# An average pool on one core: the first tile's load cut into eight transfers of 16 interleaved partitions

## The chip, the cores and the metric

The kernel runs on one core of one Trainium2 chip; its other cores are idle. The metric is the time of one execution on the device in microseconds (us), lower is better. Before the change three runs gave 334.86, 334.95 and 335.12 us, with a median of 334.95 us.

## The reference

The input x has 32 batches of 256 channels of 4096 float32 values (134.2 MB). Each row of 4096 is cut into 256 windows of 16, and each window is averaged, so the output has 32 x 256 x 256 float32 values (8.4 MB).

```python
result = np.zeros((batch, channels, output_size), dtype=np.float32)
for i in range(output_size):
    start = int(i * length / output_size)
    end = int((i + 1) * length / output_size)
    result[:, :, i] = np.mean(x[:, :, start:end], axis=-1)
```

## The kernel before, in words

Batches and channels are put together into 8192 rows of 16 KB. The kernel works through them in 16 tiles of 512 rows: 128 partitions with R = 4 rows each, so that a tile is 128 x 16384 float32 values, 8.39 MB, and each partition takes one unbroken run of 64 KB from memory. The first 15 tiles share a layout (`x_many`) in which partition p owns 60 successive rows of x and tile t takes the t-th four of them. The last tile has a layout of its own (`x_last`).

Per tile, in program order:

- SP, the engine that issues the transfers, issues the load of the tile `xin` (line 64) as one transfer over all 128 partitions. The pool `inpool` has two buffers, so tile t can't be loaded before tile t-2 has been worked off.
- POOL (line 67) adds the upper eight to the lower eight elements of each window, for the second half of the tile's windows (`m` to `cells`, 512 windows in each partition).
- DVE sums the first half's windows of 16 (line 72), and then the second half's windows of 8 that POOL has left (line 75). Both write into `res_many`, or for the last tile into `res_last`. Line 75 is the last reader of the tile, and with it the buffer comes free.
- ACT scales the tile's results by 1/16 in place (line 78).

The results of the first 15 tiles stay in `res_many` and are stored by one transfer (line 66) that SP issues behind the last load, once ACT has scaled tile 14. The last tile's results are stored at the end (line 83). All transfers, loads and stores, go through SP's one queue to the core's 16 DMA engines, in the order in which SP issues them. POOL and DVE wait for the whole tile, by the semaphores of its transfers. The framework gives each transfer one of eight semaphores in turn, and where a semaphore comes round again, it has SP wait until its last transfer has landed.

Of the kernel before, what the change touches and what calls it, by code (L numbers as in the profile page):

```python
# [1 line left out]

# [4 lines left out]


@with_exitstack
def kernel(  # L10
    ctx: ExitStack,
    tc: tile.TileContext,
    x: bass.AP,
    output_size: int,
    out: bass.AP,
):

    nc = tc.nc
    F32 = mybir.dt.float32
    X = mybir.AxisListType.X

    batch, channels, length = x.shape
    ob, oc, olen = out.shape
    assert ob == batch and oc == channels and olen == output_size
    assert length % output_size == 0
    window = length // output_size  # L30
    hw = window // 2
    inv_w = 1.0 / float(window)

    P = nc.NUM_PARTITIONS
    R = 4
    rows = batch * channels
    assert rows % (P * R) == 0
    ntiles = rows // (P * R)
    many = (ntiles - 1) * R
    cells = R * output_size  # L40
    m = cells // 2
    cols = R * length

    xr = x.rearrange("b c l -> (b c) l")
    orow = out.rearrange("b c o -> (b c) o")
    x_many = xr[0 : P * many, :].rearrange("(p r) l -> p (r l)", p=P, r=many)
    o_many = orow[0 : P * many, :].rearrange("(p r) o -> p (r o)", p=P, r=many)
    x_last = xr[P * many :, :].rearrange("(p r) l -> p (r l)", p=P, r=R)
    o_last = orow[P * many :, :].rearrange("(p r) o -> p (r o)", p=P, r=R)

    inpool = ctx.enter_context(tc.tile_pool(name="inpool", bufs=2))
    respool = ctx.enter_context(tc.tile_pool(name="respool", bufs=1))
    res_many = respool.tile([P, (ntiles - 1) * cells], F32, name="res_many")
    res_last = respool.tile([P, cells], F32, name="res_last")

    for t in range(ntiles):
        last = t == ntiles - 1
        xin = inpool.tile([P, cells, window], F32, name="xin")
        if last:
            res, base, src = res_last, 0, x_last  # L60
        else:
            res, base = res_many, t * cells
            src = x_many[:, t * cols : (t + 1) * cols]
        nc.sync.dma_start(out=xin.rearrange("p o w -> p (o w)"), in_=src)  # L64
        if last:
            nc.sync.dma_start(out=o_many, in_=res_many[:, :])
        nc.gpsimd.tensor_add(  # L67
            out=xin[:, m:cells, 0:hw],
            in0=xin[:, m:cells, 0:hw],
            in1=xin[:, m:cells, hw:window],  # L70
        )
        nc.vector.reduce_sum(  # L72
            out=res[:, base : base + m], in_=xin[:, 0:m, :], axis=X
        )
        nc.vector.reduce_sum(  # L75
            out=res[:, base + m : base + cells], in_=xin[:, m:cells, 0:hw], axis=X
        )
        nc.scalar.mul(  # L78
            out=res[:, base : base + cells],
            in_=res[:, base : base + cells],  # L80
            mul=inv_w,
        )
    nc.sync.dma_start(out=o_last, in_=res_last[:, :])


# [1 line left out]
_INS = ['x', 'output_size']  # L87
_OUTS = [((32, 256, 256), 'float32')]

_NUMBERS = {'output_size': 256}  # L90


# [26 lines left out]
```

## Time and profile before

| | |
|---|---|
| median of three runs | 334.95 us |
| the profiled execution: time | 334.98 us |
| the profiled execution: span from first to last instruction | 333.2 us |
| data moved | 134.22 MB read, 8.39 MB written |
| DMA engines busy, share of the span | 99.1% |
| DVE, POOL, ACT busy | 209.7, 139.7, 18.2 us |
| packets on the DMA queue | 2592, of them 288 under 512 B |

The span lacks 1.8 us of the execution's own time. A packet is what one DMA engine moves in one piece: each of the 16 loads and the two stores has 128 data packets, one for each partition, and one small packet on each of the 16 engines that counts up the semaphore, together 18 x (128 + 16) = 2592. "Landing" is the moment when the last of these has arrived. In the chain of waits, "DMA" is time in which the chain waits for a landing. "SPq" and "POOLq" are those engines' sequencers, and "issue" is time with no wait that the profile shows.

### The profile page before, as it was taken

Reading aid. Unit: us, or ns where it says so; the run is one execution under the profiler, and the core shown is the slowest. Engines: PE = TensorE matmul, PEld = TensorE weight load, DVE = VectorE, ACT = ScalarE, POOL = GpSimd, SP = SyncE. Lnnn points to the kernel's source line nnn. Section 1 sums busy time; section 2 is a strip of 40 time slices with the busy share of each in tenths; the row PEclk is TensorE's granted clock in tenths of the full one; section 3 lists DMA queues with packets and bytes.
Section 4 is the critical chain, followed back from the end, with each engine's and each line's share of the span. In section 5 each row is a group of like instructions: output and inputs, shape, how many; then the busy total and the mean of one; then the engine's idle time right before and its main releaser. Section 6 shows DMA issues by size and latency. Waiting matters only on the chain.

```text
span 333.2 us, 158 instructions
## 1 busy us (share of the span) xinstructions
DVE 209.7 (63%) x32; ACT 18.2 (5%) x17; POOL 139.7 (42%) x20
## 2 busy tenths in 40 slices
DVE  0029396693929569392956839295783929578491
ACT  1000101001010100001010000101010010101001
POOL 0027091642709064370906336090733609073460
DMA  9898989999898989999898989989898989989896
GB/s 378 378 504 378 496 386 456 425 417 464 378 504 378 496 386 472 409 425 456 378 504 378 504 378 456 425 378 504 378 504 378 504 378 456 425 386 496 384 450 299
DMA packets 2592, 142.61 MB, mean 428 GB/s; under 512 B 288, under 2 KB 288, under 8 KB 416
## 3 DMA queue, kind: packets, MB, share of 16 engines
q1 hardware_dynamic: 2592, 142.61, 99.1%
HBM read 134.22 MB, written 8.39 MB: 428 GB/s over the span
## 4 chain that ended last, share of the span: by engine, by line
DMA 66%; POOL 18%; DVE 11%; POOLq 3%; issue 0%; ACT 0%; SPq 0%
DMA xin<-in_x_dram 66%; POOL xin L67 18%; DVE res_many L75 9%; POOLq L114 3%; DVE res_last L75 1%; ACT res_last L78 0%; SPq L64 0%; POOLq L67 0%
## 5 line engine op out<-in xcount | busy, mean ns | idle before, releaser
L67 POOL TENSOR_TENSOR xin<-xin 128x4096 f32<-128x4096 f32 x16 | 139.5, 8717 | 181.9 <-DMA xin<-in_x_dram 181.9
L72 DVE TENSOR_REDUCE res_many<-xin 128x512 f32<-128x8192 f32 x15 | 130.3, 8686 | 107.9 <-DMA xin<-in_x_dram 107.9
L75 DVE TENSOR_REDUCE res_many<-xin 128x512 f32<-128x4096 f32 x15 | 66.3, 4420 | 2.5 <-POOL xin L67 2.3
L78 ACT ACTIVATE res_many<-res_many 128x1024 f32<-128x1024 f32 x15 | 15.8, 1056 | 290.2 <-DVE res_many L75 290.2
L72 DVE TENSOR_REDUCE res_last<-xin 128x512 f32<-128x8192 f32 x1 | 8.7, 8687 | 6.1 <-DMA xin<-in_x_dram 6.1
L75 DVE TENSOR_REDUCE res_last<-xin 128x512 f32<-128x4096 f32 x1 | 4.4, 4420 | 0.2 <-POOL xin L67 0.2
L78 ACT ACTIVATE res_last<-res_last 128x1024 f32<-128x1024 f32 x1 | 1.1, 1056 | 18.3 <-DVE res_last L75 18.3
L78 ACT ACT_TABLE_LOAD x1 | 1.3, 1283 | 0.7 <-PEq L100 0.7
L100 POOL MEMSET const-float32-0.0<- 128x1 f32 x1 | 0.1, 98 | 0.2 <-issue 0.2
L100 POOL MEMSET const-bfloat16-1.0<- 128x1 bf16 x1 | 0.1, 101 | 0.0
L100 POOL MEMSET const-uint8-127<- 128x1 uint8 x1 | 0.1, 101 | 0.0
L100 POOL MEMSET const-float32-1.0<- 128x1 f32 x1 | 0.1, 98 | 0.0
## 6 DMA issues: line engine op xcount, KB each, us to landing
out_dram<-res_many SPq DMA_DIRECT2D x1, 7680.0 KB, 23.0
out_dram<-res_last SPq DMA_DIRECT2D x1, 512.0 KB, 4.9
xin<-in_x_dram SPq DMA_DIRECT2D x16, 25.4
```

Of the source, the lines that this page charges most:

```text
L67: nc.gpsimd.tensor_add(out=xin[:, m:cells, 0:hw], in0=xin[:, m:cells, 0:hw], in1=xin[:, m:cells, hw:window],)
L72: nc.vector.reduce_sum(out=res[:, base : base + m], in_=xin[:, 0:m, :], axis=X)
L75: nc.vector.reduce_sum(out=res[:, base + m : base + cells], in_=xin[:, m:cells, 0:hw], axis=X)
L78: nc.scalar.mul(out=res[:, base : base + cells], in_=res[:, base : base + cells], mul=inv_w,)
L100: nc = _bacc.Bacc("TRN2", target_bir_lowering=False, num_devices=1)
L114: with _tile.TileContext(nc) as tc:
```

## The change

The load of tile 0 becomes eight transfers in place of one. Transfer j takes the partitions j, j+8, j+16 and so on up to j+120: 16 of the 128 partitions, one 64 KB run in each. All other loads stay as they are, and so do all instructions of POOL, DVE and ACT.

```diff
     R = 4
+    STEP = 8
...
-        nc.sync.dma_start(out=xin.rearrange("p o w -> p (o w)"), in_=src)
+        flat = xin.rearrange("p o w -> p (o w)")
+        if t == 0:
+            for j in range(STEP):
+                nc.sync.dma_start(out=flat[j:P:STEP, :], in_=src[j:P:STEP, :])
+        else:
+            nc.sync.dma_start(out=flat, in_=src)
         if last:
             nc.sync.dma_start(out=o_many, in_=res_many[:, :])
```

In the compiled program SP's list has eight copies of 16 x 16384 ahead of fifteen of 128 x 16384. The eight take all eight semaphores. So the load of tile 1, which had no wait, now waits for the first of the eight to land; the load of tile 2 waits for the other seven and, as before, for DVE; and the first instructions of POOL and of DVE wait for eight semaphores in place of one. Elsewhere the order of each engine's instructions is the same.

## Prediction

> **What bounds the kernel now.** I read the chain of waits by line first, then the two busy rows over the span, then stretches of time, and last the waits of SP and of the engines.
>
> ```profile
> DMA xin<-in_x_dram 66%; POOL xin L67 18%; DVE res_many L75 9%; POOLq L114 3%; DVE res_last L75 1%; ACT res_last L78 0%; SPq L64 0%; POOLq L67 0%
> DMA  9898989999898989999898989989898989989896
> DMA packets 2592, 142.61 MB, mean 428 GB/s; under 512 B 288, under 2 KB 288, under 8 KB 416
> q1 hardware_dynamic: 2592, 142.61, 99.1%
> ```
>
> The chain gives POOL 18% and DVE 9%, because it passes through the work that frees a buffer. The other rows say that the DMA engines are busy for 99.1% of the span, so they are the real bound. The stretches (columns: DVE, ACT, POOL busy; granted clock; DMA share; GB/s, where a packet counts at its start, so that short stretches can show a share over 1):
>
> ```profile
> 1.00:1.50 0.50, 0.00 (x0) 0.50 (x1) 0.00 (x0) 1.00 0.00 0
> 1.50:2.00 0.50, 0.00 (x0) 0.50 (x1) 0.00 (x0) 1.00 4.38 1442
> 2.00:2.25 0.25, 0.00 (x0) 0.01 (x1) 0.00 (x0) 1.00 2.28 786
> 2.25:2.50 0.25, 0.00 (x0) 0.00 (x0) 0.00 (x0) 1.00 0.70 262
> 2.50:2.75 0.25, 0.00 (x0) 0.00 (x0) 0.00 (x0) 1.00 0.74 262
> ...
> 42.09:61.44 19.35, 13.11 (x2) 1.06 (x1) 8.72 (x1) 1.00 1.00 434
> 61.44:293.67 232.23, 157.27 (x24) 12.67 (x12) 104.61 (x12) 1.00 1.00 433
> ```
>
> The queue starts between 1.5 and 2.75 us and then never rests. One load takes 19.35 us (DVE starts on tile 1 at 42.09 and on the last two tiles at 293.67 and 313.02 us). An engine moves 8 of the 128 runs in that time: 19.35 / 8 = 2.42 us for a run of 64 KB, 27.1 GB/s for each engine, 16 x 27.1 = 433 GB/s. So whatever makes one engine's line of runs longer or shorter, anywhere, moves the end by as much, unless it is less than the cover named below.
>
> **The change, part by part.**
>
> *Seven more issues on SP.* One issue of line 64 takes 328 ns as a median and 425 at most, by that line's own view; eight take 8 x 0.38 (the first one's row in the chain) = 3.0 us, against one 0.38 before. The run of transfer j is wanted by its engine only when j earlier runs are through, 2.42 us apart, and an issue takes 0.38. The queue therefore fills faster than it drains, and this costs 0. Without that cover it would be 7 x 0.38 = 2.7 us.
>
> *Semaphore packets.* 7 x 16 = 112 more, seven on each engine. The packet records of the trace, one level below the views, put each at 9 ns, and the next run starts 6 ns after it begins: 7 x 6 to 7 x 9 ns = 0.04 to 0.06 us. I take 0.05.
>
> *The start.* The stretches show 1442 GB/s x 0.5 us = 0.72 MB, or 11 runs, starting before 2.0 us, then 3, 1 and 1: 16 runs, the last 0.8 us behind the first (the records have them from 1.70 to 2.48). The last engine stays last to the end. If the descriptors of a transfer are made engine after engine, 16 runs of a small transfer are handed out sooner than 128. Bounds: a gain between 0 and 0.78 us. The trace has no transfer of this form; I take 0.15, because the early starters' first runs lasted longest (up to 3.5 us, the late ones 2.8 to 3.0), so that most of the head start was not kept.
>
> *New waits.* SP:
>
> ```profile
> SPq L64 <- DVE res_many L75: 185.8, 14, 13.3
> SPq L64 <- DMA xin<-in_x_dram: 95.3, 14, 21.2
> ```
>
> Load 1 was issued straight behind load 0; now it waits for the first of the eight, which lands about one run after the start, 1.7 + 3.1 = 5 to 7 us even if a run takes twice as long. Its own runs are wanted only when load 0 is through, at 21.7 us or later: 0, with 15 us of cover. Behind it on SP stands load 2, which waits for DVE anyway. POOL and DVE start tile 0 behind eight semaphores; a wait of this kind took 17 ns on SP and POOL's steps before its adds 0.02 and 0.09 us, so seven more are 0.1 to 0.8 us at the most, and those for early transfers pass while the last one is still under way. This delays the freeing of tile 0's buffer (35.97 us: line 75 starts at 31.55 and takes 4.42) and so the issue of load 2. But load 1 keeps the queue busy until 41 us or so (DVE starts on it at 42.09), a cover of 5 us: 0.
>
> *The run's own length.* This is the open price. Every transfer of the trace spans all 128 partitions; none shows 16 runs of which each lies eight partitions from the next. Lower bound: such a run takes 2.42 us as its nearest kin in size do, and the price is 0; nothing below, since no stretch of the trace exceeds 434 GB/s. Upper bound: the 27.1 GB/s is not the engine's pace but that of an entrance of the on-chip memory which several partitions share, and two runs of a small transfer meet in one entrance: 2 x 2.42 = 4.84 us, a load of 8 x 4.84 = 38.7 us, and a price of 19.35 us with no cover, as the DMA engines have no slack. In size the nearest row is the 2.42; in what differs, which partitions are written at once, there is no row. I take the upper end, and that is a choice. For it: the pace is the same to a per mille with every run of 230 us, which is how a fixed path looks and not a memory with traffic. For it, weakly: the only runs that set out nearly in step, the first ones, took up to 3.5 us, a few tenths of a run of which may be a start-up delay. Against it: all rows agree with an engine's own limit as well. The selection is regular, every eighth, and a regular selection meets a regular division of the memory either evenly or with whole groups left out; half of them is the least that can be left out by a step of eight over a division in powers of two.
>
> [...] The stretches show 434 GB/s with 128 partitions in one transfer. [...]
>
> **The sum.** The profiled execution's own time, 334.98 us (span 333.2 and 1.8 around it): 334.98 + 19.35 + 0.05 - 0.15 = 354.2 us. It lies 0.03 above the median of the runs, so **354.2** stands. Behind tile 0 nothing is new: load 2 is again issued some 5 us before it is wanted, all shifted by 19.35 us.
>
> **The rivals.**
>
> - *Forecast, runs doubled:* 354.2 us, 352.5 to 355.5. Chance 0.70.
> - *Fewer engines:* a small transfer is not one run per engine but sits on eight of the 16, always the same ones, two runs each at 2.42 us. The change then doesn't do what it says, and the load again takes 16 x 2.42 = 38.7 us: 354.2 as well, but with a DMA share near 0.5 in tile 0. Chance 0.03.
> - *Partly shared:* one of two engines gets ahead until they no longer meet, or they meet on half the runs: a price of about 9.7 us, 340 to 351. Chance 0.09.
> - *No sharing (the other side):* the mechanism is that a run goes at its engine's own pace wherever it lands. Place: the 8 runs of each engine in tile 0. Price 0: 334.98 + 0.05 - 0.15 = 334.9. It decides as soon as a run of a small transfer takes under 2.42 + 0.67 / 8 = 2.50 us. For it: every one of the 2304 long and short runs fits. Chance 0.14.
> - *No sharing, and a start in step:* the whole 0.78 us is won: 334.98 + 0.05 - 0.78 = 334.25, which is just over 0.2% faster. Chance 0.04.
>
> **How the numbers follow.** 0.2% is 0.67 us, about what a measurement of this kernel can tell from no change. Faster 0.04; within 0.2% 0.14; slower 0.70 + 0.03 + 0.09 = 0.82. The likeliest case's own range is 352.5 to 355.5. The range must take in both ends of the open price, so it runs from the no-sharing case, 334.4, to the doubled one, 355.5.
>
> **What would show it.** In the profile after: DVE's first start (22.76 us before) at about 42; the DMA share in the first 40 us still near 1 while GB/s there is near 217, which is sharing, or a share near 0.5, which is fewer engines; 19.35 us per tile from then on; SP's load of tile 1 issued by 7 us and the DMA share without a gap before tile 2. A first start of DVE near 22.5 would make the prediction wrong at the run's length; a gap after tile 0 would make it wrong at the waits. The packet count should be 2592 + 112 = 2704.

## The result, and the profile after

The changed kernel takes 356.19 us (median of five runs, 356.16 to 356.36) against 334.95 us for the kernel before, run beside it: a ratio of 1.0634 (95% interval 1.0618 to 1.0649). It is 21.2 us slower; the span of the profiled execution grew from 333.2 to 354.4 us. The forecast was 354.2 us, with a range that ended at 355.5.

The page of the changed kernel: the chain by line, the DMA share and the rate in 40 slices, the packets.

```profile
DMA xin<-in_x_dram 61%; POOL xin L74 20%; DVE res_many L82 9%; POOLq L121 2%; DVE res_last L82 1%; SPq L69 1%; ACT res_last L85 0%; POOLq L74 0%
DMA  9979998999999999999999999999999999999996
GB/s 237 207 148 237 237 451 377 473 436 392 473 436 392 473 436 392 473 414 414 473 407 422 473 407 422 473 399 429 473 392 436 473 392 436 473 392 436 459 444 281
DMA packets 2704, 142.61 MB, mean 402 GB/s; under 512 B 400, under 2 KB 400, under 8 KB 528
```

The share of busy time shows almost nothing: the engines are as busy as before (99.2% of the span, 99.1% before). The rate beside it shows all of it: in the first five slices (44 us) it is half, and then it is back. A run counts as busy time for as long as it takes, so runs that last twice as long leave the share at 1. The same by stretches (columns as in the prediction):

```profile
2.00:2.25 0.25, 0.00 (x0) 0.01 (x1) 0.00 (x0) 1.00 12.28 2621
2.25:2.50 0.25, 0.00 (x0) 0.00 (x0) 0.00 (x0) 1.00 7.60 1573
...
10.00:20.00 10.00, 0.00 (x0) 0.00 (x0) 0.00 (x0) 1.00 1.02 210
20.00:30.00 10.00, 0.00 (x0) 0.00 (x0) 0.00 (x0) 1.00 1.01 210
30.00:40.00 10.00, 0.00 (x0) 0.00 (x0) 0.00 (x0) 1.00 1.02 210
...
64.00:314.00 250.00, 169.79 (x26) 13.73 (x13) 112.80 (x13) 1.00 1.00 433
```

The kernel before, from 10 to 40 us:

```profile
10.00:40.00 30.00, 13.11 (x2) 1.06 (x1) 8.72 (x1) 1.00 0.99 428
```

Between 2.00 and 2.50 us 2621 x 0.25 + 1573 x 0.25 = 1049 KB start, which is 16 runs of 65.5 KB: all 16 engines have one at once. From 10 to 40 us the share is 1 and the rate 210 GB/s. The packet records, one level below the views, show the runs of load 0 at 5.10 us (2.42 before), except the fifth on each engine at 4.91 us and the first, which took 4.39 to 5.35 us. The timeline, with start, duration, engine and line:

```profile
0.73 4.98 SPq L69 DMA_DIRECT2D xin<-in_x_dram  x8
8.59 49.39 SPq L71 DMA_DIRECT2D xin<-in_x_dram  x2
44.41 8.69 DVE L79 TENSOR_REDUCE res_many<-xin 128x512 f32<-128x8192 f32 x1 [44.41 <-DMA xin<-in_x_dram]
63.42 8.69 DVE L79 TENSOR_REDUCE res_many<-xin 128x512 f32<-128x8192 f32 x1 [5.80 <-DMA xin<-in_x_dram]
```

The same two starts of DVE in the kernel before:

```profile
22.76 8.69 DVE L72 TENSOR_REDUCE res_many<-xin 128x512 f32<-128x8192 f32 x1 [22.76 <-DMA xin<-in_x_dram]
42.09 8.69 DVE L72 TENSOR_REDUCE res_many<-xin 128x512 f32<-128x8192 f32 x1 [6.12 <-DMA xin<-in_x_dram]
```

DVE starts on tile 0 at 44.41 us in place of 22.76. On tile 1 it starts at 63.42 in place of 42.09, later by 21.3 us, and that is the delay of the end. Behind tile 1 everything is as it was, with 433 GB/s and 19.35 us to a tile.

### The profile page after: what moved, and what is told of

The parts are those of the page before. It is cut to its first block, busy times and chain, and to the rows that moved or that the text cites. A ratio compares the mean times of both kernels' runs of the same rounds, so it can differ in the third digit from the quotient of the medians.

```text
span 354.4 us, 176 instructions
## 1 busy us (share of the span) xinstructions
DVE 209.7 (59%) x32; ACT 18.2 (5%) x17; POOL 139.7 (39%) x20
## 3 DMA queue, kind: packets, MB, share of 16 engines
q1 hardware_dynamic: 2704, 142.61, 99.2%
## 4 chain that ended last, share of the span: by engine, by line
DMA 61%; POOL 20%; DVE 10%; another core or an unknown queue 3%; POOLq 3%; SPq 1%; issue 0%; ACT 0%
DMA xin<-in_x_dram 61%; POOL xin L74 20%; DVE res_many L82 9%; POOLq L121 2%; DVE res_last L82 1%; SPq L69 1%; ACT res_last L85 0%; POOLq L74 0%
```

## The experiments

Three theories stood against each other. **Shared entrances** (the forecast's): several partitions share one way into the on-chip memory, and two engines whose runs meet there halve each other. No trace shows such an entrance, so the theory is judged by the rates and run lengths that it foresees. **Transfer count**: eight transfers with their semaphores cost a stall each. **Source rows**: the distance in memory between the 16 runs of a transfer (7.9 MB) slows the reading. Each experiment changes only the loop that loads tile 0.

### Sixteen neighbours to a transfer

```diff
-    nc.sync.dma_start(out=flat[j:P:STEP, :], in_=src[j:P:STEP, :])
+    nc.sync.dma_start(out=flat[16 * j : 16 * j + 16, :], in_=src[16 * j : 16 * j + 16, :])
```

> Tile 0 in eight transfers of 16 neighbouring partitions, from 16j to 16j + 15, in place of every eighth one. Three theories. Shared entrances: the runs of one transfer queue at the few entrances that its partitions share; with four runs to an entrance a run takes 4 x 2.42 = 9.7 us, or 4 x 2.55 = 10.2 us at the pace that the changed kernel's runs show (5.10 us for two), so tile 0 takes 77 to 82 us and the kernel 393 to 397 us. [...] Transfer count: each of the eight transfers costs its engines a stall, wherever its partitions lie: 356 us, as the changed kernel. Source rows: the 7.9 MB between a transfer's runs in memory is what slows it; here they are 0.98 MB apart as in the kernel before: 335 us.

Measured: 388.98 us, ratio 1.1612 (1.1591 to 1.1633). DVE's first start and the stretch before it:

```profile
77.29 8.69 DVE L81 TENSOR_REDUCE res_many<-xin 128x512 f32<-128x8192 f32 x1 [77.29 <-DMA xin<-in_x_dram]
10.00:66.00 56.00, 0.00 (x0) 0.00 (x0) 0.00 (x0) 1.00 1.03 116
```

The 116 GB/s at a full share (1.03) are about a quarter of 433. Eight transfers again, but 54 us slower instead of 21: the count is not the price. The source rows, at 0.98 MB as before, are not either. From the second on a run took 9.28 us, below the 9.67 that four runs to an entrance should give, so the size was missed. The four itself was the author's estimate; what the run shows is the quarter of the rate. The two experiments on the order, below, show where the difference lies: behind certain other sets a run is shorter, 4.91 us in place of 5.10 and 9.24 in place of 9.64. Such a run is called a passage here, because by the author's reading it goes to other entrances than the run before it; the records show its length alone.

### Two halves

```diff
-            for j in range(STEP):
-                nc.sync.dma_start(out=flat[j:P:STEP, :], in_=src[j:P:STEP, :])
+            for j in range(2):
+                nc.sync.dma_start(out=flat[64 * j : 64 * j + 64, :], in_=src[64 * j : 64 * j + 64, :])
```

> Tile 0 in two transfers, partitions 0 to 63 and 64 to 127. Shared entrances: each half reaches half of the entrances, so every run takes about 5 us, the load 8 x 4.84 to 8 x 5.10 = 39 to 41 us, the kernel 354 to 356 us. [...] Transfer count: one boundary in place of seven, 21.2 / 7 = 3.0 us: 338 us. Source rows: 0.98 MB apart as before: 335 us.

Measured: 356.31 us, ratio 1.0636 (1.0617 to 1.0656). DVE's first start:

```profile
44.29 8.69 DVE L81 TENSOR_REDUCE res_many<-xin 128x512 f32<-128x8192 f32 x1 [44.29 <-DMA xin<-in_x_dram]
```

Two transfers cost what eight cost, and the rate from 10 to 40 us was 210 GB/s again. That each half reaches half of the entrances was the author's estimate; the run shows half the rate. The runs took 5.12 us, the fifth, where the second half begins, 4.92 us.

### Eight transfers over all partitions

```diff
-    nc.sync.dma_start(out=flat[j:P:STEP, :], in_=src[j:P:STEP, :])
+    nc.sync.dma_start(out=flat[:, j * c : j * c + c], in_=src[:, j * c : j * c + c])
```

Here `c` is an eighth of the 16384 columns.

> Tile 0 in eight transfers again, but each over all 128 partitions and an eighth of the columns (2048 of 16384, runs of 8 KB). The number of transfers, their semaphores and all waits are those of the changed kernel; only the set of partitions is the whole one. Shared entrances: 334.9 to 335.5 us, the price of the seven further transfers alone (some 0.05 us for their semaphore packets, and what the longer runs list adds at the start). Transfer count: 356 us. Source rows: 335 us.

Measured: 335.21 us, ratio 1.0007 (0.9998 to 1.0016), no difference that can be told. The profile of this kernel:

```profile
13.25 8.69 DVE L82 TENSOR_REDUCE res_many<-xin 128x512 f32<-128x8192 f32 x1 [13.25 <-DMA xin<-in_x_dram]
10.00:40.00 30.00, 13.11 (x2) 1.06 (x1) 8.72 (x1) 1.00 1.06 451
```

The seven further transfers, their semaphores and the waits cost nothing visible. The cut by columns even lets DVE begin at 13.25 us, because its half of the tile is complete after four transfers, and that is worth nothing either: the DMA queue sets the end.

### The same partitions from one stretch of memory

```diff
-    nc.sync.dma_start(out=flat[j:P:STEP, :], in_=src[j:P:STEP, :])
+    nc.sync.dma_start(out=flat[j:P:STEP, :],
+                      in_=xr[64 * j : 64 * j + 64, :].rearrange("(p r) l -> p (r l)", p=16, r=R))
```

> Every eighth partition as in the changed kernel, but transfer j takes its 16 runs from one unbroken megabyte of x (rows 64j to 64j + 63) in place of runs 7.9 MB apart. Tile 0 then holds other rows of x than the reference puts there. Shared entrances and transfer count: 356 us, with runs of 5.1 us. Source rows: 335 us, with runs of 2.42 us; between the two if both matter.

Measured: 356.15 us, ratio 1.0632 (1.0612 to 1.0651).

```profile
44.51 8.69 DVE L82 TENSOR_REDUCE res_many<-xin 128x512 f32<-128x8192 f32 x1 [44.51 <-DMA xin<-in_x_dram]
```

The source of the runs doesn't matter; runs took 5.09 us. (Tile 0 holds other rows of x here, so the output is not the reference's; the amounts moved are the same.) Of the three theories only the one on the set of partitions that is written at once is left.

### Another order of the eight

```diff
-            for j in range(STEP):
+            for j in (0, 4, 1, 5, 2, 6, 3, 7):
```

> The eight transfers of the changed kernel in the order 0, 4, 1, 5, 2, 6, 3, 7 in place of 0 to 7. In the changed kernel all runs take 5.10 us but the fifth, which takes 4.91 us; it is the one at which j passes from 3 to 4. [...] In this order every run from the second on is such a passage: seven runs at 4.91 in place of one, so the load is 6 x 0.19 = 1.1 us shorter and the kernel takes 355.0 us. If the short fifth run has another cause, which goes by its place in the list, it stays the only one: 356.2 us.

Measured: 355.27 us, ratio 1.0608 (1.059 to 1.0625), so 0.9 us less than the changed kernel; the forecast of this experiment was 355.0.

```profile
43.33 8.69 DVE L79 TENSOR_REDUCE res_many<-xin 128x512 f32<-128x8192 f32 x1 [43.33 <-DMA xin<-in_x_dram]
```

DVE starts 1.1 us sooner than in the changed kernel (44.41). The records have nearly every run from the second on at 4.91 to 4.93 us (the longest 4.96). The short fifth run goes with the change from j below 4 to j from 4 on, not with its place. The author reads it as a change of entrances; the run shows the lengths.

### Every fourth and every second partition over the whole tile

```diff
-            for j in range(STEP):
-                nc.sync.dma_start(out=flat[j:P:STEP, :], in_=src[j:P:STEP, :])
+            for j in range(4):
+                nc.sync.dma_start(out=flat[j:P:4, :], in_=src[j:P:4, :])
```

> Tile 0 in four transfers of every fourth partition, 32 partitions each. [...] Shared entrances with engine e taking two successive partitions of the set (8e + j, 8e + 4 + j): at any time the 16 engines still write only half of the entrances, and change over at every run: runs of 4.91 us, 355 us. Shared entrances with each engine keeping to an entrance of its own: 2.42 us, 335 us. Cost by transfer or by the step in the partitions alone: between the two kernels, 335 + 3/7 x 21.2 = 344 us.

Measured: 335.34 us, ratio 1.0014 (1.0003 to 1.0024).

```profile
23.08 8.69 DVE L79 TENSOR_REDUCE res_many<-xin 128x512 f32<-128x8192 f32 x1 [23.08 <-DMA xin<-in_x_dram]
10.00:40.00 30.00, 13.11 (x2) 1.06 (x1) 8.72 (x1) 1.00 1.04 452
```

```diff
-            for j in range(STEP):
-                nc.sync.dma_start(out=flat[j:P:STEP, :], in_=src[j:P:STEP, :])
+            for j in range(2):
+                nc.sync.dma_start(out=flat[j:P:2, :], in_=src[j:P:2, :])
```

> Tile 0 in two transfers of every second partition, 64 partitions each. [...] Shared entrances with engine e taking four successive partitions of the set: two runs on one half of the entrances, two on the other; three passages at 4.91 us, the others at 5.10 us: 355.8 us. With each engine keeping to an entrance of its own: 335 us. A cost by transfer: 338 us.

Measured: 335.28 us, ratio 1.0012 (1.0002 to 1.0022).

```profile
22.96 8.69 DVE L79 TENSOR_REDUCE res_many<-xin 128x512 f32<-128x8192 f32 x1 [22.96 <-DMA xin<-in_x_dram]
```

Both run at the full rate (452 and 450 GB/s from 10 to 40 us), with runs of 2.42 us. So neither a step in the partitions nor part of the partitions is the trouble. If the entrances are shared, a set that reaches all of them must be dealt out so that engines don't meet; successive partitions of the set to one engine, the first reading of each expectation, is out. The two kernels take 0.4 to 0.5 us more than the kernel before. Part of it stands in the traces from the start: DVE begins tile 1 at 42.29 and 42.22 us in place of 42.09. The first run begins at 2.06 us in place of 1.73, and SP's first issue took 0.54 and 0.55 us in place of 0.38.

### Every fourth partition of one half

```diff
-            for j in range(STEP):
-                nc.sync.dma_start(out=flat[j:P:STEP, :], in_=src[j:P:STEP, :])
+            for h in (0, 64):
+                for j in range(4):
+                    nc.sync.dma_start(out=flat[h + j : h + 64 : 4, :], in_=src[h + j : h + 64 : 4, :])
```

> Tile 0 in eight transfers of 16 partitions, every fourth one of the lower 64 and then of the upper 64. [...] If a step of eight is what hurts: 335 us. [...]

Measured: 356.1 us, ratio 1.0634 (1.0613 to 1.0655).

```profile
43.94 8.69 DVE L82 TENSOR_REDUCE res_many<-xin 128x512 f32<-128x8192 f32 x1 [43.94 <-DMA xin<-in_x_dram]
10.00:40.00 30.00, 0.00 (x0) 0.00 (x0) 0.00 (x0) 1.00 1.02 210
```

With 16 partitions of 64, a step of four costs what a step of eight does over 128; with 32 partitions over all 128 it cost next to nothing. Nor does the number of partitions in a transfer decide: 64 neighbours took 356.31 us, 64 with a step of two 335.28. What counts is which partitions the set holds; that it counts by the entrances that the set reaches is the author's reading. A division into groups of eight neighbours that share an entrance is out: the changed kernel's transfers write one partition of each group, and their runs took 5.10 us all the same. The fifth run, with which the upper half begins, took 4.89 us on all 16 engines.

### Sixteen neighbours to a transfer, in another order

Against the kernel with 16 neighbours to a transfer (388.98 us, runs of 9.28 us from the second on):

```diff
-            for j in range(STEP):
+            for j in (0, 2, 1, 3, 4, 6, 5, 7):
```

> The eight blocks of 16 neighbouring partitions again, in the order 0, 2, 1, 3, 4, 6, 5, 7 in place of 0 to 7. [...] If four sharers cost nothing, 9.67 us: 390.5 us. If an entrance is faster than one engine, 9.28 us throughout: 389.0 us.

Measured: 390.9 us, ratio 1.1672 (1.1638 to 1.1706).

```profile
78.97 8.69 DVE L81 TENSOR_REDUCE res_many<-xin 128x512 f32<-128x8192 f32 x1 [78.97 <-DMA xin<-in_x_dram]
```

The second, fourth, sixth and eighth run took 9.64 us as a median, the third, fifth and seventh 9.24 to 9.25. The reading that came to 390.5 us holds: at a quarter of the rate a run takes four times 2.41 us, without a loss. The 390.5 counts four runs at 9.67 us in place of 9.28; that there are four was the author's estimate, and the records have four, at 9.64. The short runs stand where a block follows its neighbour (2 to 1, 3 to 4, 6 to 5); in the first order every block from the second on does, so its 9.28 us are read as passages.

### Shorter runs

```diff
+            h = cols // 2
             for j in range(STEP):
-                nc.sync.dma_start(out=flat[j:P:STEP, :], in_=src[j:P:STEP, :])
+                for c in (0, h):
+                    nc.sync.dma_start(out=flat[j:P:STEP, c : c + h], in_=src[j:P:STEP, c : c + h])
```

> The changed kernel's eight sets of every eighth partition, each in two transfers of half the columns: 16 transfers with runs of 32 KB in place of 64. It asks what the 0.26 us is by which a run of 5.10 us exceeds twice 2.42. If the entrance loses a share of its pace when two engines write to it, a run takes 2.55 us, the load is as long as before, 356.2 us. If each run pays it once, whatever its length, a run takes 2.42 + 0.26 = 2.68 us, and the kernel 356.2 + 8 x 0.26 = 358.3 us.

Measured: 356.15 us, ratio 1.0634 (1.0603 to 1.0665).

```profile
44.29 8.69 DVE L83 TENSOR_REDUCE res_many<-xin 128x512 f32<-128x8192 f32 x1 [44.29 <-DMA xin<-in_x_dram]
```

From the second on, runs of 32 KB took 2.55 to 2.57 us, except the passage (the ninth) at 2.38. The loss beyond twice 2.42 us is a share of the pace (5%), not a price for each run. Sixteen transfers cost what eight and two cost.

## Why the prediction was wrong, and where it was right

**The step that failed** is the upper bound of "the run's own length": "two runs of a small transfer meet in one entrance: 2 x 2.42 = 4.84 us". It took sharing to be free of loss, so what was called a bound was none. Measured: seven runs of 5.10 and one of 4.91 us, 40.6 us in place of 38.7. This alone is 1.9 us and puts the time past the range's end of 355.5. The half of the rate that the mechanism foresaw was there: 210 GB/s at a share of 1.01 to 1.02. But no run shows an entrance, nor that two runs meet in one; what the runs showed in place of the 4.84 us are these lengths.

The sum, against the records of the engine that ended load 0 last:

| term | predicted, us | measured, us |
|---|---|---|
| runs of load 0: 7 x 5.10 + 4.91 - 8 x 2.42 | +19.35 | +21.25 |
| start-up in the first run (2.96 - 2.42 before, 5.35 - 5.10 after) | not in the sum | -0.29 |
| this engine's start (2.51 before, 2.30 after) | -0.15 | -0.21 |
| seven more semaphore packets, by the gaps between the runs | +0.05 | +0.04 |
| first run of load 1 (2.42 before, 2.78 after) | not in the sum | +0.36 |
| sum | +19.25 | +21.15 |

The start of load 2's first run on this engine is later by 21.15 us, as the sum has it, and the end of the kernel by 21.2. All terms but the first differ from the prediction by less than half a microsecond.

- *What bounds the kernel:* right. The delay at tile 1, 21.3 us, is the delay of the end; nothing absorbed it.
- *Issues on SP:* the cost of 0 was right, its rows were not. An issue took 589 ns as a median (563 to 589), not 0.38 us, although its transfer is an eighth as large. Eight took 4.98 us, still well ahead of the runs. The line of the eight issues, with their shortest, median and longest duration in ns, and that of the kernel before:

```profile
L69 SPq DMA_DIRECT2D xin<-in_x_dram x8: 563/589/589, 0.7 to 5.1; - x8
L64 SPq DMA_DIRECT2D xin<-in_x_dram x16: 327/328/425, 0.7 to 287.6; - x16
```

- *The start:* the 16 first runs set out within 0.36 us in place of 0.78, as was argued, but the first of them came 0.34 us later (2.07 in place of 1.73), so the last one set out only 0.08 us sooner. The engine that ended load 0 last was another: it set out at 2.30, and its first run took longest. The column experiment started at 1.74, so seven more issues don't delay the start. The prediction read the starts before as 1.70 to 2.48; the records have 1.73 to 2.51, and its own stretches show the last start after 2.50.
- *New waits:* right, and by the cover named. SP's own waits:

```profile
SPq L71 <- DVE res_many L82: 185.9, 14, 13.3
SPq L71 <- DMA xin<-in_x_dram: 111.9, 18, 19.9
```

The wait for DVE stayed as it was (185.8 before). Load 1 was issued at 8.59 us, later than the 5 to 7 that were foreseen, and wanted only at 42. POOL and DVE started tile 0 some 1.2 us behind its last run (0.4 before), more than foreseen, and the 5 us of cover took it.

- *The rivals:* "no sharing" and "no sharing, and a start in step" fell with the runs of 5.10 us. "Fewer engines" fell with the 16 runs that start between 2.00 and 2.50 us and a share of 1.02. Nor do the runs fit an engine for each entrance, at which two runs would queue. In the order 0, 4, 1, 5 the first two transfers reach different entrances, if its short runs (4.91 to 4.93 us) are read as changes of entrances, and all eight were issued by 5.7 us; on engines of their own they would have run side by side, and yet the rate was 210 GB/s. "Partly shared" fell too: from the second on all runs of an engine were about twice as long, and the one passage is shorter by 0.19 us only.
- *The weak argument* from the first runs of the kernel before (up to 3.5 us) was not one: the first runs of the two kernels at the full rate, every second and every fourth partition, are as long (up to 3.4 us), and their later runs take 2.42 us. So the length of a first run is no sign of sharing.
- *The range:* its lower end, 334.4, is called the no-sharing case, but that case comes to 334.9 by its own sum, and with a start in step to 334.25. Nothing hung on it.

The sets fall into three groups by what was measured. Every eighth partition, each half and every fourth of a half ran at half the rate (210 GB/s from 10 to 40 us), 16 neighbours at a quarter (116 GB/s from 10 to 66 us), every second and every fourth of the whole at the full rate (450 and 452 GB/s from 10 to 40 us). The runs show rates and lengths and no entrances: how many a set reaches is an estimate from these rates, and which partition goes to which entrance, and which engine takes which run of a transfer, was not shown.

**What stays open:** why a run at half the rate loses 5% (5.10 for 4.84 us) and one at a quarter nothing (9.64 for 9.67). That it goes with bytes and not with runs is shown (32 KB runs took 2.55 to 2.57 us); the cause is not.

Why a passage shortens a run is open as well. A reason that the author assumed: the earlier of two engines is alone on the next entrance for as long as it is ahead. With a lead of d us at the pace of one (2.42 us a run) and the rest at that of two (5.10), a run would take 5.10 - 1.1 d, so every pair that took 4.89 us would need a lead of 0.19 us. With every fourth partition of one half all 16 fifth runs took 4.89 us, but the earliest of them set out 0.11 us ahead of the next and 0.23 us ahead of the third. So the reason doesn't hold as it stands. What the experiments on the order show is which runs are short, and that rests on measured lengths alone.

## What to carry to other kernels

When a transfer is cut, ask which partitions are written at once, not only how many bytes and engines each piece has: a cut by columns, or one into sets of every second or every fourth partition of the whole, was free within 0.15%, while three cuts by partitions that looked just as even (every eighth, two halves, every fourth of a half) doubled the load's time. Read the DMA share only beside the GB/s; here a share of 1.01 to 1.02 stood beside 210 GB/s, half the rate, because the runs took 5.10 us in place of 2.42. And where every engine of a bound resource has a price that no row shows, let the range reach past the simple multiple, as sharing itself may cost something (here 5.10 us for twice 2.42).

## What the runs showed of the hardware that was not expected

- A run of 64 KB took 2.42 us at the full rate (27.1 GB/s for an engine), 5.10 us at half and 9.64 us at a quarter, passages apart. If one, two and four runs go through an entrance at once, an estimate from the ratios of these lengths (1, 2.1 and 4.0), that is 27.1, 25.7 and 27.2 GB/s for an entrance.
- An issue on SP took longer for a part of the tile than for the whole, and not by size: 328 ns as a median for the whole tile, 589 ns for 16 partitions with a step of eight, 558 ns for 64 neighbours, 420 ns for 16 neighbours, 459 ns for an eighth of the columns. Where the first issue took 0.54 to 0.58 us, the first run began at 2.06 to 2.10 us; where it took 0.38 to 0.39 us, at 1.73 to 1.76 us. The reason is open.
- Behind load 0 the engines closed up: the starts of their runs lay up to 1.2 us apart during load 0 and up to 0.56 us from the second run of load 1 on, and the first run of load 1 took 2.78 to 3.39 us.
